# Output projection: its weight loads issued from ScalarE's queue

## Chip, cores and metric

One core of one Trainium2 chip runs the whole program. The metric is the device time of one execution in microseconds, the median of the runs shown.

## What is computed

One layer of a hybrid decoder for 2048 tokens of width 1024, in fp32. Cut to what matters here:

```python
hn = rms_norm(h, pre_mix_norm);  proj = hn @ w_in
o_a = gated_head_norm(gated_delta_rule_chunked(q, k, v, g, beta), gdn_norm, z)   # 4 heads of 128
o_b = gated_head_norm(hgrn2_chunked(q, k, i, log_f), hgrn_norm, g)               # 4 heads of 128
mix = concatenate([o_a, o_b])                       # (2048, 1024)
mix_out = mix @ w_out                               # the output projection
h = h + rms_norm(mix_out, post_mix_norm)
u = rms_norm(h, pre_mlp_norm) @ w_mlp_up            # MLP, 4096 wide
h = h + rms_norm(square(relu(u)) @ w_mlp_down, post_mlp_norm)
h = h + rms_norm(p @ w_ple_proj, ple_norm) * sigmoid(h @ w_ple_gate)
```

The change touches the loads of `w_out` alone.

## The kernel before

Everything is held transposed, channels on the 128 partitions and tokens along the free dimension, in four token quarters q of 512. Products are made to about fp32 precision with three matmuls per 128-channel block: each operand x is split into a high part (rounded to fp32r, ScalarE, `split` line 164) and the rest (VectorE, line 165), and high*high, high*low and low*high are summed in PSUM.

The order of TensorE's instructions is written out by hand for the whole program (`manual_schedule`). For the other engines a scheduler orders the instructions of the first part of the program, the output projection included, from its own estimate of when each is ready; SyncE's order is by hand in the mixing loop and again from the MLP on (line 1406), and left to the scheduler in between. Each engine, and each engine's DMA queue, takes its instructions in order: one that waits holds up those behind it. SyncE issues nearly all DMAs and computes nothing. GpSimd issues 16 accumulating ones.

The stages around the change:

- The end of the mixing: the last heads' recurrences (small matmuls with copies by ScalarE and VectorE between them), interleaved with the embedding projections (`mme`, copy `e` at line 307, store `ed` at line 309).
- The output projection, L1354 on: 32 tiles `(q, d)`, 8 columns d of 128 for each of 4 quarters q, 24 matmuls each (`mmo`, line 1143, the first two tiles at line 1100). Its moving operand `mixT` is loaded from DRAM (line 327) and split in place (lines 217 and 218). Each result is copied out by ScalarE (`yo`, L1392) and squared (`sq_o`, L233) for the norm that follows.
- Its weights: for q = 0 to 2 (`RAW = 3`) `stage_out(j)` loads a 128x1024 block of 512 KB into a `raw` buffer (two of them, line 338), and `ready_out(j)` splits it into a `whl` buffer (three of them). For q = 0 it also stores the split block to a DRAM cache (`keep`, line 180). For q = 3 `ready_out` reloads the split block, 1 MB, from the cache (`reload`, line 185), with no engine's work. In the loop over tiles, `ready_out(j + 2)` and `stage_out(j + 3)` come ahead of tile j's matmuls.
- The norms after each quarter: `hl` split, two `nrm` matmuls (lines 1174 and 1175), Ln and Exp on ScalarE with a table load before each (lines 1179, 1180), VectorE steps, then for q = 0 and 1 the residual: GpSimd's accumulating DMA adds x to `yo` (L1229), ScalarE squares the sum (`sq_h`, L233; `acc_h`, L226) and SyncE stores it (`h1d`, L1232). For q = 2 and 3 `yo` is stored (`yod`, L1396).
- The first operands of the MLP (`be`, `b`, `t`) are prepared while the last tiles run.

`reload` also serves the input projection, where its calls are unchanged.

Of the kernel before, what the change touches and what calls it, by code (L numbers as in the profile page):

```python
# [10 lines left out]
F32 = mybir.dt.float32  # L11
# [77 lines left out]
def trunk(ctx, tc, x, xT, pT, vecs, w_in, w_ab, gdn_a_log, gdn_dt_bias, w_out, w_up, w_down,  # L89
          w_ple, w_gate, consts, out):  # L90
    nc = tc.nc
    V, S, G, PE = nc.vector, nc.scalar, nc.gpsimd, nc.tensor
# [69 lines left out]
    def split(t, eng, raw):  # L162

        S.activation(t[:, 0], raw, AF.Copy)  # L164
        eng.tensor_tensor(t[:, 1], raw, t[:, 0], ALU.subtract)  # L165
# [9 lines left out]
    cached, sumd = {}, {}  # L175

    def keep(key, w):

        c = dr.tile([P, 2 * KD * P], F32, name=f"cache_{key}")
        nc.sync.dma_start(c, w.bitcast(F32).rearrange("p h k n -> p (h k n)"))  # L180
        cached[key] = c

    def reload(key, name):
        w = wp.tile([P, 2, KD, P], F32R, tag="whl", name=f"w_{name}")
        nc.sync.dma_start(w.bitcast(F32).rearrange("p h k n -> p (h k n)"), cached[key])
        return w

    def gemm(ps, terms):
# [143 lines left out]
    order = [(q, d) for q in range(NQ) for d in range(KD)]  # L332
    staged_out, ready, RAW = {}, {}, 3

    def stage_out(j):
        if j < len(order) and order[j][0] < RAW:
            raw = wp.tile([P, KD, P], F32, tag="raw", name=f"raw_out{j}", bufs=2)
            nc.sync.dma_start(raw, w_out[order[j][1]])
            staged_out[j] = raw

    def ready_out(j):
        if j >= len(order):
            return
        if j not in staged_out:
            ready[j] = reload(f"out{order[j][1]}", f"out{j}")
            return
        ready[j] = wp.tile([P, 2, KD, P], F32R, tag="whl", name=f"w_out{j}")
        split(ready[j], V, staged_out.pop(j))
        if order[j][0] == 0:
            keep(f"out{order[j][1]}", ready[j])  # L350
# [84 lines left out]
    with mixers as mctx:  # L435
# [538 lines left out]
        def split_work(j):  # L974

            if j < len(works):
                split_w[j] = staged.pop(j)() if j in staged else reload(works[j][1], works[j][0])
# [74 lines left out]
        with tc.manual_schedule(engines={mybir.EngineType.SP}):  # L1052
# [5 lines left out]
            for j, (name, key, src, q, h, then, g, b) in enumerate(works):  # L1058
# [4 lines left out]
                w, xt = split_w.pop(j), xts[q]  # L1063
# [20 lines left out]
            accs, store = {q: None for q in qs}, None  # L1084
            at(clock[0], mix_operands(0), (1, 2, 3, 4, 6, 7, 9, 11))
            call(clock[0] + 2, partial(stage_out, 0))
            call(clock[0] + 5, partial(ready_out, 0))
            call(clock[0] + 6, partial(stage_out, 1))
            call(clock[0] + 13, partial(ready_out, 1))
            call(clock[0] + 14, partial(stage_out, 2))  # L1090
            held = {}

# [261 lines left out]
    for j, (q, d) in enumerate(order):  # L1354
        if d == 0:
# [3 lines left out]
            if q == 1:  # L1359
                later(mix_operands(3), range(17, 25))  # L1360
        ready_out(j + 2)
        stage_out(j + 3)
        if j == len(order) - 5:
# [391 lines left out]
    for half in range(2):  # L1755
# [4 lines left out]
        for d in range(KD):  # L1760
            w = gated.pop((half, d))
# [70 lines left out]
```

## Time and profile before

| | us |
|---|---|
| median of 3 runs | 2715.93 |
| lowest and highest | 2712.65, 2716.56 |
| the profiled execution, first to last instruction (span) | 2719.9 |

The profiled execution's time is its span; nothing more than the span is given for it, and it lies 4.0 us above the median. Times in the prediction's rows count from the start of that span. The output projection runs from about 1113 to 1314 us. Rows of a timeline give start, duration, engine, line, operation, destination and source, and in brackets how long the engine stood idle before and what released it. `SPq` is SyncE's DMA queue; a row of it is the issue of a DMA, not its transfer. `xN` counts instructions that are merged in a row.

### The profile page before, as it was taken

To read this page: it belongs to the slowest core of one execution; us is meant where nothing else is said; L and a number is where in the kernel's file an instruction comes from. 1 tells how busy PE (TensorE), PEld (TensorE's weight loads), DVE (VectorE), ACT (ScalarE), POOL (GpSimd) and SP (SyncE) were. 2 spreads that over 40 slices of the span, in tenths; PEclk is the share of its full clock that TensorE was granted. 3 is DMA by queue.
4 is the path that set the end of the run, shared out by engine and by line. 5 is a ranking of instruction groups with operands and counts; after the bars stand their busy time and mean duration, and the time that the engine had idled before them with its cause. 6 is when DMAs were issued, how large, how long until landed. Compare 5 with 4: busy or idle time off the path is not lost.

```text
span 2719.9 us, 38475 instructions
## 1 busy us (share of the span) xinstructions
PE 2660.8 (98%) x12745; PEld 2215.1 (81%) x12745; DVE 2040.8 (75%) x4219; ACT 1464.0 (54%) x2940; POOL 118.5 (4%) x133
## 2 busy tenths in 40 slices
PE   8999999999999999998999999999999999999999
PEld 6788888888888887876788888888888888888887
DVE  7778878787777777576989867768787765567776
ACT  7665555465445455575655646555555545465432
POOL 0000000000000000011000000001000000001000
PEclk9999999999999999998999999999999999999999
DMA  8777777667666665887566457667454346577663
GB/s 282 273 237 255 236 263 242 216 214 241 213 201 221 223 213 164 271 281 231 177 232 228 175 178 240 216 202 244 164 196 163 139 172 207 193 256 247 216 212 131
DMA packets 268742, 589.24 MB, mean 217 GB/s; under 512 B 55658, under 2 KB 60232, under 8 KB 249344
## 3 DMA queue, kind: packets, MB, share of 16 engines
q1 hardware_dynamic: 266240, 582.59, 63.9%
q0 software_dynamic: 2304, 4.20, 0.9%
q8 instruction: 101, 1.65, 0.3%
q14 instruction: 97, 0.79, 0.1%
HBM read 419.75 MB, written 166.92 MB: 216 GB/s over the span
## 4 chain that ended last, share of the span: by engine, by line
PE 51%; DMA 3%; DVE 3%; issue 3%; ACT 1%; POOL 1%; SPq 0%; POOLq 0%; DVEq 0%; ACTq 0%
PE d L1143 22%; PE u L1143 22%; PE mmg L1143 6%; PE mmo L1143 1%; DMA raw_out<-in_w_out_dram 1%; DMA yo<-in_xT_dram 0%; PE mme L191 0%; POOL acc_y L234 0%; DMA b<-h1d 0%; DMA w_out<-cache_out 0%; DMA db<-hid 0%; DVE t L165 0%; DMA h1d<-yo 0%; POOL yo L1229 0%; DVE pr_g L698 0%
## 5 line engine op out<-in xcount | busy, mean ns | idle before, releaser
L1072 PE MATMUL mm<-xt,w 128*128 128x512 f32 x3072 | 784.1, 400 | 1.4 <-ACT zt_zg L577 1.1
L1072 PEld LDWEIGHTS mm<-xt,w 128*128 128x128 f32 x3072 | 553.3, 189 | 102.3 <-ACT zt_zg L577 1.5
L1143 PE MATMUL d<-db,da 128*128 128x512 f32 x2688 | 611.0, 389 | 0.5 <-ACT db L217 0.2
L1143 PE MATMUL u<-t,wu 128*128 128x512 f32 x2604 | 591.1, 389 | 0.0
L1143 PEld LDWEIGHTS d<-db,da 128*128 128x128 f32 x2688 | 504.3, 188 | 106.4 <-DVE db L218 1.0
L1143 PEld LDWEIGHTS u<-t,wu 128*128 128x128 f32 x2604 | 488.7, 188 | 101.5
L218 DVE TENSOR_TENSOR db<-db 128x512 fp32r<-128x512 f32 x224 | 159.9, 714 | 72.4 <-ACT db L217 71.7
L1495 DVE TENSOR_TENSOR u<-u,u 128x512 f32<-128x512 f32 x224 | 150.2, 681 | 58.1 <-PE u L1143 56.6
L1143 PE MATMUL mmo<-mixT,w_out 128*128 128x512 f32 x720 | 173.4, 402 | 11.8 <-DMA w_out<-cache_out 5.5
L217 ACT ACTIVATE db<-db 128x512 fp32r<-128x512 f32 x224 | 140.9, 629 | 78.2 <-DMA db<-hid 71.9
L1143 PEld LDWEIGHTS mmo<-mixT,w_out 128*128 128x128 f32 x720 | 139.5, 195 | 44.6 <-DMA w_out<-cache_out 5.9
L1143 PE MATMUL mmg<-h2T,wg 128*128 128x512 f32 (+1 forms) x792 | 174.8, 383 | 0.0
L1538 ACT ACTIVATE u<-u 128x512 f32<-128x512 f32 x128 | 80.8, 631 | 166.3 <-DVE u L1495 166.0
L1143 PEld LDWEIGHTS mmg<-h2T,wg 128*128 128x128 f32 x792 | 145.5, 188 | 29.1
L165 DVE TENSOR_TENSOR da<-da 128x512 fp32r<-128x512 f32 x128 | 93.7, 732 | 77.7 <-ACT da L164 77.1
L164 ACT ACTIVATE da<-da 128x512 fp32r<-128x512 f32 x128 | 80.5, 629 | 124.8 <-DMA da<-sumd 91.6
L164 ACT ACTIVATE wu<-a 128x512 fp32r<-128x512 f32 x124 | 75.0, 623 | 44.3 <-DMA a<-in_w_up_dram 43.0
L698 DVE TENSOR_TENSOR pr_g<-xs_g,sys_g 128x16 f32<-128x16 f32 (+14 forms) x240 | 94.4, 393 | 5.6
L165 DVE TENSOR_TENSOR wu<-a,wu 128x512 fp32r<-128x512 f32 x124 | 85.6, 693 | 10.8 <-ACT wu L164 10.5
L234 POOL TENSOR_TENSOR acc_y<-acc_y,sq_y 128x512 f32<-128x512 f32 x28 | 38.5, 1374 | 1261.6 <-ACT sq_y L233 1260.8
L1539 ACT ACTIVATE u<-u 128x512 f32<-128x512 f32 x128 | 80.5, 629 | 3.1
L165 DVE TENSOR_TENSOR da<-dr,da 128x512 fp32r<-128x512 f32 x96 | 66.3, 691 | 19.0 <-ACT da L164 16.5
(385 smaller groups left out, 3792.6 us busy)
## 6 DMA issues: line engine op xcount, KB each, us to landing
w<-cache_in SPq DMA_DIRECT2D x96, 1024.0 KB
db<-hid SPq DMA_DIRECT2D x224, 256.0 KB
cache_in<-w SPq DMA_DIRECT2D x32, 1024.0 KB
hid<-u SPq DMA_DIRECT2D x128, 256.0 KB
da<-sumd SPq DMA_DIRECT2D x128, 256.0 KB
a<-in_w_up_dram SPq DMA_DIRECT2D x124, 256.0 KB
hid<-ht SPq DMA_DIRECT2D x96, 256.0 KB
dr<-in_w_down_dram SPq DMA_DIRECT2D x96, 256.0 KB
```

The source lines that it names most:

```text
L164: S.activation(t[:, 0], raw, AF.Copy)
L165: eng.tensor_tensor(t[:, 1], raw, t[:, 0], ALU.subtract)
L217: S.activation(t[:, 0], plain(t), AF.Copy)
L218: V.tensor_tensor(t[:, 1], plain(t), t[:, 0], ALU.subtract)
L234: eng.tensor_tensor(acc, acc, sq, ALU.add)
L698: V.tensor_tensor(pr[:, :, :, 0:i], xs[:, None, :, 0:i].broadcast_to([P, 2, GC, i]), sys[:, 0:i, i : i + 2].rearrange("p j two -> p two j" ...
L1072: PE.matmul(ps, *terms[i], start=i == 0, stop=i == nt - 1)
L1143: PE.matmul(ps, a, b, start=start, stop=stop)
L1495: V.tensor_tensor(c[new], c[old], ps, ALU.add)
L1538: S.activation(c[k], c[k], AF.Relu)
L1539: S.activation(c[k], c[k], AF.Square)
```

## The change

All loads of the output projection's weights are issued by ScalarE: the 24 whole blocks in `stage_out` (512 KB each) and the 8 reloads of cached split ones in `ready_out` (1 MB each). `S` is `nc.scalar`. Addresses, sizes, buffers and splits stay.

```diff
-    def reload(key, name):
+    def reload(key, name, queue=None):
         w = wp.tile([P, 2, KD, P], F32R, tag="whl", name=f"w_{name}")
-        nc.sync.dma_start(w.bitcast(F32).rearrange("p h k n -> p (h k n)"), cached[key])
+        (queue or nc.sync).dma_start(w.bitcast(F32).rearrange("p h k n -> p (h k n)"), cached[key])
         return w
...
     def stage_out(j):
         if j < len(order) and order[j][0] < RAW:
             raw = wp.tile([P, KD, P], F32, tag="raw", name=f"raw_out{j}", bufs=2)
-            nc.sync.dma_start(raw, w_out[order[j][1]])
+            S.dma_start(raw, w_out[order[j][1]])
             staged_out[j] = raw
...
         if j not in staged_out:
-            ready[j] = reload(f"out{order[j][1]}", f"out{j}")
+            ready[j] = reload(f"out{order[j][1]}", f"out{j}", S)
             return
```

TensorE's and GpSimd's orders come out the same as before. ScalarE's has 32 rows more, SyncE's 32 less and some of its other DMAs, the `mixT` loads above all, stand earlier; on ScalarE and VectorE some instructions around the loads change places.

## The prediction

> **What bounds the kernel now.** I read the page first, then the time by windows around the output projection, then who waited for whom on TensorE, then the timelines of SyncE, ScalarE, VectorE and TensorE side by side. Tiles of the output projection are counted j = 8q + d, 0 to 31; j = 0 to 23 are loaded whole and split, j = 24 to 31 come back split from the cache.
>
> ```profile
> span 2719.9 us, 38475 instructions
> PE 2660.8 (98%) x12745; PEld 2215.1 (81%) x12745; DVE 2040.8 (75%) x4219; ACT 1464.0 (54%) x2940; POOL 118.5 (4%) x133
> 1060.00:1080.00 20.00, 16.66 (x85) 13.75 (x84) 15.98 (x40) 9.51 (x20) 0.00 (x0) 0.94 0.25 64
> 1140.00:1160.00 20.00, 20.00 (x90) 16.47 (x88) 8.73 (x12) 8.03 (x14) 1.01 (x1) 1.00 0.93 334
> 1160.00:1180.00 20.00, 17.63 (x71) 13.96 (x70) 11.77 (x16) 16.83 (x25) 0.00 (x0) 0.91 0.85 299
> 1240.00:1260.00 20.00, 16.67 (x61) 12.91 (x60) 15.12 (x23) 11.40 (x20) 4.52 (x6) 0.83 1.03 274
> 1260.00:1280.00 20.00, 14.53 (x53) 11.49 (x52) 5.10 (x9) 8.54 (x13) 0.00 (x0) 0.83 0.82 301
> PE mmo L1143 <- DMA w_out<-cache_out: 5.5, 1, 5.5
> PE mmo L1143 <- DVE w_out L165: 3.3, 3, 2.2
> PE mmo L1143 <- ACT w_out L164: 2.9, 2, 1.8
> SPq L338 <- DVE w_out L165: 19.2, 9, 3.6
> ```
>
> The window rows give length, then busy time and count of PE, PEld, DVE, ACT and POOL, the granted clock, the DMA share and GB/s. TensorE is busy 98% of the span, so only its gaps can be won or made. The undisturbed stretch 1140 to 1160 holds 90 matmuls, 0.222 us each and 5.33 us for a tile's 24. The three disturbed stretches hold 71, 61 and 53, so they lose 19, 29 and 37 matmuls: 4.2, 6.4 and 8.2 us, 18.8 us in all. That is more than the waits (11.7 us) because the granted clock falls to 0.91 and 0.83 beside them. 18.8 us is 0.7% of the span, the most that this stage can give. All three waits are for the weights whose loads are moved. The last row shows how they come late: SyncE's queue stood 19.2 us at the loads (L338), for VectorE to free the buffer.
>
> **The change part by part.** The compared orders show TensorE and GpSimd unchanged. 32 issues leave SyncE, 24 of 512 KB and 8 of 1 MB, and stand in ScalarE's order; the scheduler also moves the mixT loads ahead on SyncE and reorders some splits on ScalarE and VectorE.
>
> *The issues themselves.* No trace row shows an issue from ScalarE; the nearest are the same ones from SyncE.
>
> ```profile
> L338 SPq DMA_DIRECT2D raw_out<-in_w_out_dram x24: 332/414/1615, 1076.6 to 1239.6; - x24
> L185 SPq DMA_DIRECT2D w_out<-cache_out x8: 319/399/1712, 1258.2 to 1298.5; - x8
> ```
>
> At the medians 24 x 0.414 + 8 x 0.399 = 13.1 us of ScalarE over some 220 us; at the longest 1.6 and 1.7 us, 52 us. It is 54% busy, and the windows above leave it idle 3 to 12 us in 20, so I put the issues themselves at nothing; the waits and places below carry the price. Every whole load waits for VectorE's subtraction of the tile two earlier. On ScalarE that wait now holds the copies (yo), squares and splits queued behind it, for about one subtraction (1.2 us), less where mixT splits stand between.
>
> *Tile 8, the first gap.*
>
> ```profile
> 1147.40 1.23 DVE L165 TENSOR_TENSOR w_out<-raw_out,w_out 128x1024 fp32r<-128x1024 f32 x1 [1.59 <-ACT w_out L164]
> 1153.43 1.61 SPq L338 DMA_DIRECT2D raw_out<-in_w_out_dram  x1
> 1161.02 1.06 ACT L164 ACTIVATE w_out<-raw_out 128x1024 fp32r<-128x1024 f32 x1
> 1162.13 0.73 PE L1143 MATMUL mmo<-mixT,w_out 128*128 128x512 f32 x2 [1.85 <-ACT w_out L164]
> 1163.39 10.35 PE L1143 MATMUL mmo<-mixT,w_out 128*128 128x512 f32 x38 [0.53 <-DVE w_out L165]
> ```
>
> The buffer for tile 8 was free at 1147.40 + 1.23 = 1148.6, but SyncE, in order, came to the load at 1153.4. In the new order the load stands right behind ScalarE's copy of tile 6 and waits for this subtraction alone. The loads before it also go out sooner (tile 2's sits in ScalarE's order before the third embedding copy, near 1071). Walking the rows, tile 8 goes out near 1147 instead of 1153.4. A load then took 7.6 us to its copy, so the copy can begin near 1155, and with 2.3 us for copy and subtraction the weights are ready at 1157, before TensorE ends tile 7 at 1160.3. The gap closes: -4.2 us. Bounds: 0 (the load lands 4 us later) and -4.2 us.
>
> *Tile 23, the second gap.* Its cause is not the issue:
>
> ```profile
> 1247.54 0.63 ACT L233 ACTIVATE sq_h<-yo 128x512 f32<-128x512 f32 x1 [4.73 <-DMA yo<-in_xT_dram]
> 1249.03 1.06 ACT L164 ACTIVATE w_out<-raw_out 128x1024 fp32r<-128x1024 f32 x1
> 1253.12 7.86 PE L1143 MATMUL mmo<-mixT,w_out 128*128 128x512 f32 x22 [2.25 <-DVE w_out L165]
> ```
>
> The copy of tile 23 stands on ScalarE behind a square that waits for GpSimd's accumulating DMA, and the new order keeps it there. I put this at nothing, with -6.4 us (the gap goes) and +1.5 us (that DMA shares the engines with one queue more) as ends, the latter about the third of the 4.73 us that one competitor more of three would take.
>
> *Tiles 24 to 31, the third gap.*
>
> ```profile
> 1252.40 0.58 ACT L1392 ACTIVATE yo<-mmo 128x512 f32<-128x512 f32 x1
> 1258.18 0.42 SPq L185 DMA_DIRECT2D w_out<-cache_out  x1
> 1266.44 6.65 PE L1143 MATMUL mmo<-mixT,w_out 128*128 128x512 f32 x16 [5.47 <-DMA w_out<-cache_out]
> 1273.58 0.63 ACT L164 ACTIVATE hl_o<-acc_o 128x512 fp32r<-128x512 f32 x1 [5.38 <-PE nrm_h L1175]
> 1279.01 0.59 ACT L226 ACTIVATE acc_o<-mmo 128x512 f32<-128x512 f32 x1
> 1283.10 0.63 ACT L1179 ACTIVATE r_o<-acc_o 128x512 f32<-128x512 f32 x1 [2.21 <-DVE acc_o L1178]
> 1287.71 0.62 ACT L164 ACTIVATE t<-b 128x512 fp32r<-128x512 f32 x1
> ```
>
> TensorE ends tile 23 at 1253.12 + 7.86 = 1260.98. The reload of tile 24 went out at 1258.18 and let it go on at 1266.44, L = 8.26 us. Now it stands behind the copy and square of tile 21: about 1253.9. Idle before tile 24 is then L - 7.1. The later reloads are worse placed than on SyncE. Tile 27's stands behind the norm's Ln and Exp: from hl_o to the end of acc_o is 6.0 us, and hl_o waits for the norm's matmuls, 16 matmuls into tile 24 (1265.0), so it issues at 1271.0 where tile 27 is due at 1277.9: idle L - 6.9. Tile 28's stands behind the second Ln and Exp, from 1279.60 to 1287.71, 8.1 us and one issue later: 1279.5, with tile 28 due at 1283.2: idle L - 3.7, less what tile 27 has idled. Tiles 25, 26 and 29 to 31 have two tiles' time, 10.7 us, less some 2 us of ScalarE, which covers L up to about 8.5 us.
>
> L is the unknown. From below it is the fastest 512 KB load, plus its second half at the 301 GB/s of the row above (1.7 us); from above the slowest 512 KB load:
>
> ```profile
> 1163.36 0.33 SPq L338 DMA_DIRECT2D raw_out<-in_w_out_dram  x1
> 1166.85 1.06 ACT L164 ACTIVATE w_out<-raw_out 128x1024 fp32r<-128x1024 f32 x1 [0.60 <-DMA raw_out<-in_w_out_dram]
> 1194.45 0.67 SPq L338 DMA_DIRECT2D raw_out<-in_w_out_dram  x1
> 1204.74 1.06 ACT L164 ACTIVATE w_out<-raw_out 128x1024 fp32r<-128x1024 f32 x1 [1.53 <-DMA raw_out<-in_w_out_dram]
> ```
>
> That is 3.5 + 1.7 = 5.2 us and 10.3 us. I take the middle of 5.2 and 8.26, 6.7 us, since the reload no longer stands behind SyncE's stores. Idle is then 3.0 us, all before tile 28. The old gap lost 8.2 us for 5.47 idle, 1.5 for 1, so 3.0 costs 4.5: -3.7 us. At L = 5.2 it is -6.0, at 8.26 +0.5 (idle 5.8), at 10.3 +6.5 us (idle 9.8).
>
> The Trainium skill, page "DMA: Bandwidth & Descriptors", section "Issuing engines are not separate DMA queues", holds that DMAs from several engines share the same 16 DMA engines and that issuing from more of them only saves sequencer time. By it L would stay at the old value and the third gap would not shrink. No run so far tells the two apart: this trace has SyncE's queue and GpSimd's alone, and the 3.5 to 10.3 us are from one queue.
>
> *The end of the mixing.*
>
> ```profile
> 1067.45 0.43 ACT L826 ACTIVATE hb_h<-qk_h 128x256 f32<-128x256 f32 x1 [2.54 <-DVE qk_h L824]
> 1070.26 0.33 SPq L708 DMA_DIRECT2D xd_g<-xs_g  x1
> 1070.63 0.42 SPq L309 DMA_DIRECT2D ed<-e  x1
> 1074.83 0.60 ACT L307 ACTIVATE e<-mme 128x512 f32<-128x512 f32 x1 [4.32 <-DMA ed<-e]
> 1076.28 0.71 PE L853 MATMUL at_h<-qk_h,keys_h 128*128 128x128 f32 x4 [1.88 <-ACT keys_h L858]
> 1085.22 1.23 DVE L165 TENSOR_TENSOR w_out<-raw_out,w_out 128x1024 fp32r<-128x1024 f32 x1
> ```
>
> The loads of tiles 0 and 1 now go out near 1061. Tile 0's copy falls into ScalarE's idle 2.54 us before 1067.45 if the load lands in 3.5 us; if it takes 7.6, that cover is gone and the copies behind it slip by 1.6 us. Its subtraction (1.23 us) moves from 1085 into the solve that ends with the store xd_g, so xd_g, the store ed behind it on SyncE, the e copy and the keys behind that slip by about 0.9 us, and TensorE's 1.88 us wait grows by as much; at 1085 VectorE has 0.5 us less, since another split moves ahead there. Sum between -0.5 and +2.2, taken at +1.0 us.
>
> **Sum.** +1.0 - 4.2 + 0 - 3.7 = -6.9 us. The profiled span is 4.0 us above the median of the runs, 2715.93; the stage's difference is taken over to that median: 2709.0 us. About 0.2%, 5.4 us, is what a measurement of this kernel can tell from no change.
>
> **The rivals.** *Slower: the reloads wait behind ScalarE's own chain.* If reloads take as long as the slowest load, L = 10.3, tiles 24, 27 and 28 idle 3.2 + 3.4 + 3.2 us: +6.5; with the upper ends of mixing (+2.2) and tile 23 (+1.5) and tile 8's -4.2 it is +6.0, 2721.9 us. It decides from L = 8.2 up. For it: tile 28's issue 3.7 us before it is due. Against it: the DMA share of 0.82 and the clear queue.
>
> *No change: the DMA engines bound it.* The shares of 0.93, 0.85 and 1.03 speak for it; mixT loads move ahead into 1120 to 1160 and fill what was free. Tile 8's gap then stays, L = 8.26 (+0.5), mixing +1.0: +1.5, 2717.4 us. The rule of the Trainium skill above is this rival. Against it: tile 8 had its buffer 4.8 us before its load went out.
>
> *More: tile 23's gap goes too,* if the accumulating DMAs land earlier because SyncE's loads are out of the way: -6.9 - 6.4 = -13.3, 2702.6 us. Against it: the same bytes move in a window at 1.03.
>
> **How the numbers follow.** Forecast 0.45, slower 0.25, no change 0.17, more 0.13. The forecast's own range, -2 to -10 us, lies two thirds past -5.4: 0.31 faster, 0.14 same. "More" gives 0.13 faster; "no change" 0.02, 0.13, 0.02; "slower" 0.02 same, 0.23 slower. Together 0.46 faster, 0.29 same, 0.25 slower. Cases of both signs hold much, so the range goes past both outer ones by 3 us or so: 2699 to 2725; the likeliest alone 2706 to 2714.
>
> **What would show it.** Right: a second hardware queue of 20 MB, L338 and L185 on ScalarE's queue, 85 or more matmuls in the 20 us around tile 8, a wait of under 1 us before tile 24 and one of 2 to 4 us before tile 28. Wrong: the waits before tiles 24 to 28 sum over 6 us, a wait for w_out at tile 8, ScalarE standing for VectorE at L338 while TensorE waits for a free bank, or the end of the mixing losing over 3 us.

## Result and the profile after: slower by 0.29%

The changed kernel takes 2722.6 us, the median of 13 runs (2718.5 to 2728.2), the kernel before 2713.6 (2709.8 to 2720.0) beside it: ratio 1.0029 (the two medians alone give 1.0033), 95% interval 1.0021 to 1.0037, 5.7 to 10.0 us slower. 2709.0 and "faster" were forecast. The profiled execution of after took 2723.15 us, 1.85 more than its span. Medians of before differ by up to 10 us from one set of runs to the next, so below only ratios within a set are compared.

The page of after, and who waited for whom on TensorE and ScalarE between 1060 and 1340 us (total us, times, longest):

```profile
span 2721.3 us, 38491 instructions
q10 hardware_dynamic: 4608, 20.97, 2.4%
L338 ACTq DMA_DIRECT2D raw_out<-in_w_out_dram x24: 334/335/397, 1055.2 to 1242.9; - x24
PE mmo L1143 <- DVE w_out L165: 7.4, 3, 3.4
PE mmo L1143 <- DMA w_out<-cache_out: 5.4, 2, 5.0
PE psb_g L769 <- DVE r_g L766: 3.0, 1, 3.0
PE nrm_o L1174 <- ACT hl_o L164: 1.7, 3, 1.1
ACT yo L1392 <- DVE w_out L165: 5.9, 2, 5.0
ACT L1179 <- DVE w_out L165: 1.8, 1, 1.8
ACT hl_o L164 <- DVE w_out L165: 1.7, 1, 1.7
```

The change does what it says: a second hardware queue moves 21 MB, and an issue costs 0.335 us. New are a wait of the recurrence's `psb_g` for VectorE, and three kinds of waits of ScalarE for VectorE's weight splits, which are ScalarE standing at its own loads.

The spans differ by 1.4 us only, because after's execution came 4.8 us earlier to the first `mme` (1059.32 against 1064.12), in a part that the change leaves alone; over all the profiles below it comes between 1057.9 and 1067.4. So I count from there: the start of the first `mme`, then the start of the first matmul of tile n of the output projection (matmul 24n + 1 of `mmo`; all 768 are in every trace), then the last matmul of a norm in this stage (`nrm_o`, L1175; 1325.06 in before). The first line is in us from the first `mme`; the others are differences from it, so the change from one column to the next is what that stretch lost. Where TensorE waits for VectorE's half of a tile's weights, it does so ahead of that tile's third matmul, so such a wait counts in the next column. Single profiles of one order differ: e3 keeps before's order up to tile 23 and reads up to 2.2 us lower, e14 up to tile 9 and reads up to 1.0 us higher.

| kernel | tile 0 | 2 | 7 | 9 | 15 | 17 | 21 | 23 | 25 | norm |
|---|---|---|---|---|---|---|---|---|---|---|
| before | 49.1 | 63.3 | 90.6 | 105.8 | 138.9 | 150.3 | 173.5 | 186.0 | 211.1 | 260.9 |
| after | +3.0 | +4.0 | +4.0 | +3.3 | +5.3 | +5.7 | +8.9 | +7.7 | +5.2 | +6.4 |
| e1 | +2.3 | +3.3 | +3.3 | +1.5 | +4.8 | +8.0 | +8.1 | +6.8 | +7.7 | +7.6 |
| e2 | -0.8 | -0.8 | -0.8 | +0.7 | +1.2 | +1.2 | +1.7 | +0.1 | -5.2 | -3.9 |
| e3 | -1.9 | -1.9 | -1.9 | -1.9 | -1.9 | -1.9 | -1.0 | -2.2 | -0.8 | -0.2 |
| e4 | +3.7 | +3.2 | +3.9 | +1.9 | +7.5 | +8.7 | +9.8 | +9.1 | +1.7 | +11.4 |
| e5 | -0.4 | -0.6 | -0.6 | -2.3 | -2.3 | -2.3 | -1.4 | -2.4 | -1.2 | -0.4 |
| e6 | -0.7 | +0.3 | +0.3 | -3.8 | -0.9 | +1.4 | +5.6 | +4.0 | -0.2 | +0.1 |
| e7 | -0.9 | +2.0 | +3.1 | -1.3 | -1.3 | +1.0 | +3.6 | +1.9 | +0.3 | +0.5 |
| e8 | +6.4 | +6.0 | +7.1 | +4.8 | +9.6 | +10.0 | +12.6 | +10.9 | +11.5 | +13.3 |
| e9 | +1.9 | +3.4 | +3.4 | +0.1 | +2.5 | +3.3 | +6.6 | +4.9 | +3.4 | +4.1 |
| e10 | -1.0 | +0.2 | +0.2 | +1.7 | +5.1 | +5.8 | +9.1 | +7.4 | +6.1 | +6.8 |
| e11 | +1.2 | +1.6 | +4.2 | +7.9 | +7.9 | +7.9 | +7.7 | +6.5 | +7.2 | +6.9 |
| e12 | -0.1 | +0.3 | +2.8 | +6.7 | +6.7 | +6.7 | +6.8 | +5.1 | +0.3 | +0.9 |
| e13 | -0.5 | +1.8 | +1.8 | -2.5 | -0.6 | +2.6 | +2.4 | +1.5 | +0.1 | +0.5 |
| e14 | +0.8 | +0.8 | +1.0 | +1.0 | +1.0 | +1.0 | +4.5 | +2.9 | +1.6 | +2.2 |
| e15 | -0.8 | +0.7 | +0.7 | -3.7 | -0.8 | +2.4 | +5.0 | +3.5 | -0.3 | -0.5 |

After loses 3.0 us by tile 0 and 1.0 behind it; it wins 0.7 from tile 7 to 9, loses 2.0 on the way to 15, 0.4 to 17 and 3.2 from 17 to 21; it wins 3.7 from 21 to 25 and loses 1.2 to the end: 6.4 us, beside 7.9 measured.

### The profile page after: what moved, and what is told of

It reads as the page before. It is cut to its first block, busy times and chain, and to the rows that moved or that the text cites. A ratio compares the mean times of both kernels' runs of the same rounds, so it can differ in the third digit from the quotient of the medians.

```text
span 2721.3 us, 38491 instructions
## 1 busy us (share of the span) xinstructions
PE 2657.6 (98%) x12745; PEld 2212.0 (81%) x12745; DVE 2040.5 (75%) x4219; ACT 1463.6 (54%) x2940; POOL 119.3 (4%) x133
## 4 chain that ended last, share of the span: by engine, by line
PE 56%; DVE 5%; DMA 4%; issue 4%; ACT 1%; POOL 1%; SPq 0%; POOLq 0%; DVEq 0%; ACTq 0%
PE u L1143 22%; PE d L1143 21%; PE mmg L1143 6%; PE mm L1072 4%; PE mmo L1143 1%; DVE pr_g L698 1%; POOL acc_y L234 0%; DMA rsb_g<-rd_g 0%; DMA mixT<-mixd 0%; DVE t L165 0%; PE mme L191 0%; DMA sys_g<-ud_g 0%; DVE xs_g L701 0%; DMA yo<-in_xT_dram 0%; DMA ud_g<-u_g 0%
```

## The experiments

### Which loads: e1 to e4

The `raw` load is issued from ScalarE where the condition holds, else from SyncE (e1 `j < KD`, e2 `j >= KD`); `reload` stays on SyncE in both. e3 is the reverse. e4 takes GpSimd for all.

```diff
-            S.dma_start(raw, w_out[order[j][1]])
+            (S if j < KD else nc.sync).dma_start(raw, w_out[order[j][1]])     # e1
+            (nc.sync if j < KD else S).dma_start(raw, w_out[order[j][1]])     # e2
+            nc.sync.dma_start(raw, w_out[order[j][1]])                        # e3, reload on S
+            G.dma_start(raw, w_out[order[j][1]])                              # e4, reload on G
```

> Only the eight whole weights of the first block of 512 tokens are loaded from ScalarE's queue; the other sixteen and the cached ones stay on SyncE's. Theory A (order): the two first loads, free of SyncE's order, land some 20 us earlier, the scheduler then puts their splits ahead of the operands of the mixing's end, and SyncE's freed places go to later transfers ahead of the last heads' norms; most of the loss sits here, from the trace of after 3.0 us at the end of the mixing, 1.0 at a low clock behind it and little at the tiles 7 and 8: slower by 3 to 6 us, about 2718. Theory B (ScalarE stands at each load until VectorE has freed the buffer): a third of the loads, a third of the loss, some 2 to 3 us. Theory C (a second hardware queue slows the small transfers of SyncE's): about 2 us, where both queues are busy at the end of the mixing.

Measured: 1.0036 (1.0023 to 1.0048). The first eight alone lose as much as the whole change, more than the 3 to 6 us expected, but in part elsewhere: 3.3 us by tile 2, and 6.5 us from tile 9 to 17, where after loses 2.4.

> Only the sixteen whole weights of the second and third block are loaded from ScalarE's queue; the first eight and the cached ones stay on SyncE's. Theory A: no order of the mixing's end is touched, so the 4 us there are not lost, and what is left is ScalarE held ahead of the rows of the norms and of tile 20, 1 to 3 us slower in the trace of after, less up to 3 us if the gap before tile 23 closes: within 2 us of before. Theory B: two thirds of the loads, so about 5 us slower. Theory C: about 4 us slower.

Measured: 0.9992 (0.9983 to 1.0001). The later sixteen lose nothing, against B and C.

> Only the eight cached split weights are loaded from ScalarE's queue; all whole ones stay on SyncE's. Theory A: the order changes only from tile 23 on; in the trace of after tile 24 still waited 5.0 us, and the stretch from tile 23 to tile 32 was 3.1 us shorter than before: 0 to 3 us faster, about 2712. Theory B: the first load stands behind a copy that waits for its buffer's store, nothing gained, 0 to 1 us slower. Theory C: 1 to 2 us slower, all three waits of tiles 24, 27 and 28 longer by the second queue's landings.

Measured: 1.0008 (0.9999 to 1.0017). No gain; the reload still came late (below).

> All 32 loads are issued from GpSimd's queue, which does little else here; ScalarE issues none. SyncE is freed of them just as in after, so the order of SyncE and most of that of VectorE is new in the same way. Theory A: the loss stays for the most part, slower than before by 3 to 8 us, unless the first splits come where they were. Theory B: ScalarE no longer stands at a load, so the loss goes: within 2 us of before or faster by up to 7. Theory C: the loads still run on a queue of their own, slower by 4 to 8 us.

Measured: 1.0067 (1.0053 to 1.0081), the worst of all. With nothing issued by ScalarE the loss is larger, and 3.7 us of it are lost by tile 0 with a wait of 1.5 us for `r_g`, so ScalarE's standing is not the whole of it. GpSimd stands in its turn: 87.8 us in 18 waits at the loads, for VectorE's subtractions. Its own instructions are not held up by that: every power step of the norms (`m_h`, `m_e`, `m_g`) in this stage begins within 0.3 us of the end of VectorE's step before it. The profile shows 11.4 of the 18 us measured in this stage, 9.7 of them behind tile 25, where TensorE waits 5.9 us for the split of a weight of the MLP (`w_u`); why that comes late was not taken apart.

### Why the first loads cost: e5 to e8

At the end of the mixing the two kernels agree until the last 2 us: `mme` 15 of 16 (groups of six matmuls) begins 0.2 us earlier in after than in before, counted from the first. Then VectorE of after, and of before:

```profile
1104.77 0.16 DVE L280 TENSOR_SCALAR m_e<-m_e 128x4 f32<-128x4 f32 x1
1108.36 0.75 DVE L593 SCALAR_TENSOR_TENSOR og_g<-og_g,cols,rsb_g 128x512 f32<-128x512 f32 x1 [3.43 <-DMA rsb_g<-rd_g]
1110.23 0.34 DVE L766 SCALAR_TENSOR_TENSOR r_g<-vt_g,inv_g,psa_g 128x128 f32<-128x128 f32 x1
1110.63 0.49 PE L769 MATMUL psb_g<-r_g,xt_full 128*128 128x128 f32 x2 [3.01 <-DVE r_g L766]
```

```profile
1111.33 0.35 DVE L766 SCALAR_TENSOR_TENSOR r_g<-vt_g,inv_g,psa_g 128x128 f32<-128x128 f32 x1
1112.64 0.75 DVE L593 SCALAR_TENSOR_TENSOR og_g<-og_g,cols,rsb_g 128x512 f32<-128x512 f32 x1 [0.96 <-DMA rsb_g<-rd_g]
```

In before the recurrence's `r_g` comes first and the norm's product `og_g`, which waits for the landing of `rsb_g`, after it. In after they have changed places, and TensorE stands 3.01 us. Nothing in the diff names either. Counted from the first `mme`, the loads of the first two weights go out 16.6 and 28.8 us sooner and the first weight's subtraction comes 16.2 us sooner, and the scheduler places the rest anew by its estimates; e5 shows that the early loads alone are enough to turn the pair.

```diff
# e5, from before                            # e8, from after, in ready_out
-  call(clock[0] + 2, partial(stage_out, 0))  +  if j == 0:
+  stage_out(0)                               +      V.tensor_copy(ready[0][:, 0, 0, :1],
-  call(clock[0] + 6, partial(stage_out, 1))  +                    xin[0][1][:, 0, :1])
+  stage_out(1)                                  split(ready[j], V, staged_out.pop(j))
# e6, from after; e7 has the reloads on SyncE besides
+  (nc.sync if j < 3 else S).dma_start(raw, w_out[order[j][1]])
```

> The kernel before, all loads on SyncE's queue, with its first two whole weights issued at the start of the mixing's end instead of 2 and 6 steps later. No second queue and no load on ScalarE. VectorE's order then has the norm's product og_g, which waits for rsb_g, ahead of the recurrence's r_g, as in after; in the kernel before r_g comes first. Theory A (order): the stretch from the first mme to tile 0, 49.1 us before, 48.2 and 47.2 in the two runs that kept its order, 51.4 to 52.8 where the first eight loads moved, takes 50 to 52 us, with a wait of 1.5 to 3 us for r_g at its end; the kernel is slower by 1 to 5 us, about 2717. Theory B (ScalarE stands at the loads) and theory C (a second hardware queue): none of it, 47 to 49 us, within 1.5 us of before.

Measured: 0.9999 (0.9990 to 1.0007), 48.7 us to tile 0. A miss for theory A in size: `og_g` stands ahead of `r_g` here too, but its row had nearly landed.

```profile
1114.16 0.75 DVE L593 SCALAR_TENSOR_TENSOR og_g<-og_g,cols,rsb_g 128x512 f32<-128x512 f32 x1 [1.23 <-DMA rsb_g<-rd_g]
1114.83 0.34 DVE L766 SCALAR_TENSOR_TENSOR r_g<-vt_g,inv_g,psa_g 128x128 f32<-128x128 f32 x1
1115.23 0.49 PE L769 MATMUL psb_g<-r_g,xt_full 128*128 128x128 f32 x2 [0.91 <-DVE r_g L766]
```

So the bad order is not enough; the price is how late the landing is behind it, 0.9 us here and 3.0 in after. From `rsb_g`'s issue to its use took 4.7 us here, 4.6 in before, 5.6 in after and 4.9 to 5.2 in e1, e4, e6 and e7, of which e6 and e7 had no load on a second queue yet: for this row a longer landing beside a second queue (C) is at most 1 us and not shown.

> As after, but the first three whole weights are loaded from SyncE's queue as before; the other 21 and the cached ones stay on ScalarE's. Theory A: the order at the end of the mixing is that of before, so 47 to 49 us to tile 0 and no wait for r_g; the later stretch as in after, which lost 2.4 us from tile 2 on, so 0 to 3 us slower than before, about 2716. Theory B: 21 of 24 loads still stand on ScalarE, so six or seven of the eight us stay, 2721. Theory C: likewise 5 to 8 us.

Measured: 1.0007 (0.9998 to 1.0016), 48.4 us to tile 0 and no wait for `r_g`. With the first three loads back on SyncE, some 6 of the 7.9 us are gone (1.0029 to 1.0007): 3.7 us by tile 0 and 3.4 from tile 7 to 9 in the table.

> As the one from tile 3 on, with the cached weights back on SyncE's queue. Theory A: the gap before tile 24 shrinks as in the run of the later sixteen alone (1.6 us against 5.5), worth 4 to 6 us, and tiles 7 and 8 may lose or win 2: 1 to 5 us faster than before, about 2712. Theory B: 5 to 7 us slower. Theory C: 3 to 6 us slower.

Measured: 0.9993 (0.9984 to 1.0002). By the two ratios the cached loads cost some 4 us on ScalarE's queue, but the intervals overlap and the two profiles end within 0.4 us of each other: not shown.

> After, with one more instruction: the first weight's split is held until the second mixing operand is split, by a copy of one column (128x1) into the weight's place. All loads stay on ScalarE's queue and as early as in after, but VectorE's order has r_g ahead of og_g again. Theory A: the wait of 3.0 us for r_g at the end of the mixing goes and the stretch from the first mme to tile 0 takes 48 to 50.5 us instead of 52.1; the kernel is 2 to 4 us faster than after, still 3 to 6 slower than before. Theories B and C: both causes stay, 51 to 53 us and no faster than after.

Measured: 1.0035 (1.0023 to 1.0047), 55.5 us to tile 0 (+6.4). The wait for `r_g` went as expected, the time did not: another waiting row of the same kind took its place.

```profile
1115.39 0.17 DVE L280 TENSOR_SCALAR m_e<-m_e 128x4 f32<-128x4 f32 x1 [3.59 <-DMA m_e<-sd_e]
1116.07 0.34 DVE L778 SCALAR_TENSOR_TENSOR S_g<-S_g,cd_g,psc_g 128x128 f32<-128x128 f32 x1
1116.47 0.49 PE L766 MATMUL psa_g<-S_g,y_kg 128*128 128x128 f32 x2 [1.77 <-DVE S_g L778]
```

VectorE waits for `m_e` ahead of `S_g`; 16 us earlier it waited 2.57 us for `rsb_h` in the same way. TensorE's wait of 1.77 us is only part of the 6.4; the rest was not taken apart. Since every edit gives the scheduler's order a new form, the theory is tested better by taking the waiting instruction off VectorE.

### Taking the waiting instruction away: e9 to e12

```diff
-            V.scalar_tensor_tensor(og, og, col(...), rsb, ALU.mult, ALU.mult)
+            if n in ("g3_2",):            # e9; e10 to e12: ("g3_2", "h3_3", "g3_3")
+                G.tensor_tensor(og, og, rsb, ALU.mult)
+                G.tensor_scalar(og, og, col(...), None, ALU.mult)
+            else: ...
```

e9 and e10 start from after, e11 from before, e12 from e2.

> After, with one product moved: og_g of head 2 in the last block, the instruction that waits for rsb_g ahead of r_g in VectorE's order, is done on GpSimd as two instructions (128x512 by the row, then by the column of gains). All 32 loads stay on ScalarE's queue. Theory A2 (the loss at the end of the mixing is VectorE standing in order at an instruction that waits for a landing, ahead of the recurrence): the 3.0 us wait for r_g goes, 48 to 50.5 us from the first mme to tile 0 where after had 52.1, and the kernel is 2 to 5 us faster than after, 1.001 to 1.002 of before. Theory B (ScalarE standing at its loads) and theory C (small transfers land later beside a second queue, 5.6 us from issue to use for rsb_g against 4.6 before): the wait turns up elsewhere, 51 to 53 us, and the ratio stays 1.003.

Measured: 1.0012 (1.0001 to 1.0022), 4.6 us less than after by the two ratios. To tile 0 it took 51.0 us, half a microsecond over what was expected, but the wait is gone:

```profile
1113.86 0.35 DVE L770 SCALAR_TENSOR_TENSOR r_g<-vt_g,inv_g,psa_g 128x128 f32<-128x128 f32 x1 [1.35 <-PE psa_g L768]
1115.04 0.39 PE L773 MATMUL psb_g<-r_g,xt_full 128*128 128x128 f32 x2
1116.31 1.29 POOL L594 TENSOR_TENSOR og_g<-og_g,rsb_g 128x512 f32<-128x512 f32 x1 [2.66 <-DMA rsb_g<-rd_g]
1116.43 2.26 DVE L165 TENSOR_TENSOR w_out<-raw_out,w_out 128x1024 fp32r<-128x1024 f32 x1 [0.26 <-ACT w_out L164]
```

VectorE has `r_g` done 2.1 us before GpSimd has its row and begins the product, and TensorE doesn't wait. From the start of the last group of six `mme` to tile 0 the kernel after loses 3.2 us against before, e9 0.1 and e10 0.1: so much is the product's. The 1.9 us that e9 still loses by tile 0 come from the solve ahead of it, a slip that after had and made up. By the table only 1.1 us of e9's gain on after stand at tile 0 and 0.6 at tile 2; most of it, 2.6 us, comes from tile 7 to 9, where the last head's row took 4.0 us from issue to use (6.8 in after), an instruction that e9 leaves where it was. So the 4.6 us are not the price of this one product alone.

> After, with the three last such products of the last block (heads g 2, h 3 and g 3) on GpSimd. Theory A2: besides the wait for r_g, the gap at tile 7 (3.4 us for VectorE's subtraction, which stood behind og_g waiting 4.3 us) falls under 1.5 us; together 4 to 7 us faster than after, 1.000 to 1.002 of before. Theory B: the copies and rows held by ScalarE remain, no more than 2 us gained on after. Theory C: the landings stay late, so the second operands are late too; no more than 2 us gained.

Measured: 1.0039 (1.0025 to 1.0052). At the end of the mixing the whole loss is gone (48.1 us to tile 0, -1.0), as A2 says, and the wait at tile 7 is 0.49 us instead of 3.39; then TensorE waits 4.96 us before tile 9, and by tile 15 5.1 us are lost. SyncE, which stands at the store of GpSimd's product with the `mixT` loads behind it, holds ScalarE for 10 us, and tile 9's split stands behind that:

```profile
1163.44 0.32 SPq L599 DMA_DIRECT2D mixd<-og_g  x1
1170.30 1.31 ACT L217 ACTIVATE mixT<-mixT 128x512 fp32r<-128x512 f32 x2 [10.01 <-DMA mixT<-mixd]
1173.58 6.64 PE L1147 MATMUL mmo<-mixT,w_out 128*128 128x512 f32 x14 [4.96 <-ACT w_out L164]
```

> The kernel before, all loads on SyncE's queue, with the same three products on GpSimd. Every other order stays as before but for one neighbouring pair on VectorE. Theory A2: the wait of 5.3 us for rsb_h and of 1.5 for rsb_g leave VectorE's order, so the splits of tiles 3 to 8 come earlier and the gap at tile 8 (1.9 and 0.5 us, with a low clock behind it) goes at least in part: 1 to 4 us faster than before. Theories B and C say nothing of VectorE's order here: the load on SyncE and its landing set tile 8, within 1 us of before.

Measured: 1.0030 (1.0017 to 1.0042): a miss, for the same reason. GpSimd and SyncE of e11:

```profile
1160.72 1.30 POOL L594 TENSOR_TENSOR og_g<-og_g,rsb_g 128x512 f32<-128x512 f32 x1 [7.97 <-DMA rsb_g<-rd_g]
1162.12 2.94 POOL L595 TENSOR_SCALAR og_g<-og_g,cols 128x512 f32<-128x512 f32 x1
1156.95 0.32 SPq L180 DMA_DIRECT2D cache_out<-w_out  x1
1165.09 0.32 SPq L599 DMA_DIRECT2D mixd<-og_g  x1
1173.76 6.56 PE L1147 MATMUL mmo<-mixT,w_out 128*128 128x512 f32 x20 [5.32 <-ACT w_out L164]
```

GpSimd ends the product at 1165.06, where VectorE takes 0.75 us for it. SyncE stands from 1157 to 1165 at its store, with loads of weights and operands behind it, and TensorE waits 5.3 us for `w_out` at tile 8. The wait was not removed but moved from VectorE's order to SyncE's.

> The later sixteen whole loads on ScalarE's queue, the first eight and the cached ones on SyncE's, and the three products on GpSimd. If the gains add up: the later sixteen alone measured 0.9992 of before, with tile 24's wait 1.6 us instead of 5.5, and the products 1 to 4 us more: 3 to 7 us faster than before, 0.9975 to 0.999. If GpSimd's products delay the stores of the mixed rows so that the last block's operands are late, or tile 23's wait of 3.5 us takes up the gain: within 2 us of before.

Measured: 1.0011 (0.9998 to 1.0023). No sum of gains; TensorE waits 5.0 us in the middle of tile 8, for a split of `mixT`.

### Tiles 7 to 21: e13 to e15

The conditions for ScalarE are `3 <= j < 8`, `16 <= j`, and both, with the reloads on SyncE.

> Only the whole weights of tiles 3 to 7 are loaded from ScalarE's queue, all others from SyncE's. Theory D (ScalarE standing at a load until VectorE has freed its buffer costs where a norm's row or a split is queued behind it): tiles 8 to 23 are not on ScalarE, so the 2.5 us that the runs from tile 3 on lost between tiles 15 and 21 are gone (under 1 us), while the gap at tile 8 closes (3 us won between tiles 7 and 9): 1 to 4 us faster than before. Theory E (the scheduler's new order of the residual's squares and stores is what costs there): the 2.5 us stay or turn up elsewhere, within 1.5 us of before.

Measured: 1.0009 (1.0001 to 1.0018). 1 to 4 us faster was expected. From 17 to 21 nothing is lost (-0.2), against 3.2 in after and 2.6 to 4.2 in e6, e7 and e15. The gap at tile 8 closes (-4.3 from 7 to 9). But 3.2 us go from 15 to 17, where tile 16's weights come late; e1, e6, e7 and e15 lose 2.3 to 3.2 us there too, after 0.4. That loss was not taken apart.

> Only the whole weights of tiles 16 to 23 are loaded from ScalarE's queue. Theory D: the norm of the second quarter falls between these loads, so 1 to 2 us are lost between tiles 16 and 21; freed of them, SyncE comes to the reload of tile 24 earlier and the gap before it shrinks by 2 to 5 us: within 3 us of before, rather faster. Theory E: no loss between tiles 16 and 21, 2 to 5 us faster.

Measured: 0.9997 (0.9988 to 1.0006); 3.5 us lost from 17 to 21. This is theory D, with ScalarE of e14 showing it:

```profile
1221.72 0.33 ACTq L338 DMA_DIRECT2D raw_out<-in_w_out_dram  x1
1222.11 0.63 ACT L164 ACTIVATE hl_o<-acc_o 128x512 fp32r<-128x512 f32 x1 [1.67 <-DVE w_out L165]
1222.79 0.50 PE L1174 MATMUL nrm_o<-hl_o,ones 128*128 128x512 f32 x1 [1.52 <-ACT hl_o L164]
```

The load waits for VectorE to free its buffer; the norm's split `hl_o`, right behind it, goes out 0.4 us after it, and TensorE waits 1.52 us for that. After's rows at 1219 are the same (1.67 us, and 1.14 at TensorE). But the loads alone don't make the loss. e2 has tiles 16 to 23 on ScalarE too and loses 0.5 us from 17 to 21; in its order the norm's split stands behind no load that waits:

```profile
1214.71 0.62 ACT L164 ACTIVATE hl_o<-acc_o 128x512 fp32r<-128x512 f32 x1
1217.40 0.50 PE L1175 MATMUL nrm_o<-hl_o,ones 128*128 128x512 f32 x1 [0.17 <-DVE hl_o L165]
```

> The whole weights of tiles 3 to 7 and 16 to 23 are loaded from ScalarE's queue. If the parts add up: 3 us at tile 8, 2 to 5 us at tile 24, less 1 to 2 us between tiles 16 and 21: 3 to 6 us faster than before, 0.998 to 0.999. If not, within 2 us of before as the run of tiles 3 to 23 was (0.9993).

Measured: 1.0006 (0.9997 to 1.0015). The parts come out in the stage, -4.4 from 7 to 9 and -5.3 from 21 to 25, but +6.1 from 9 to 17 and +2.6 from 17 to 21 take the gain up. No version beat the kernel before by more than its interval; e2 and e7, 0.9992 and 0.9993, came nearest.

## Why the prediction was wrong, step by step

The prediction summed to -6.9 us, the profile of after shows +6.4: 13.3 us apart. In the table 3.0 of them lie at the end of the mixing, up to tile 2 (+4.0 for +1.0), 3.5 at tile 8 (-0.7 for -4.2), 5.6 from tile 9 to 21 (+5.6 for 0) and 1.2 from there to the end (-2.5 for -3.7). So three steps failed.

**The end of the mixing (+1.0, at most +2.2) failed in its path.** It lost 3.0 us, and 1.0 more behind it, while the first eight matmuls of tile 0 took 3.24 us at a granted clock of 0.56 where the same eight take 1.98 us at tile 1 at 1.00:

```profile
1111.42 3.24 PE L1100 MATMUL mmo<-mixT,w_out 128*128 128x512 f32 x8
1120.11 1.98 PE L1100 MATMUL mmo<-mixT,w_out 128*128 128x512 f32 x8
```

The prediction followed the early split into the solve, and that slip did happen (+2.2 us at the seventh group of `mme`) and was made up again. What it did not follow is the order that the scheduler gave to `og_g` and `r_g` behind it, which stood in the compared orders all along. e9 and e10 show it: with the one product off VectorE the 3.2 us between the last `mme` and tile 0 are gone.

**Tile 8 (-4.2, bound 0): the mechanism holds, the forecast doesn't.** Where the first three loads stay on SyncE and those of tiles 3 to 7 move, the gap closes, -4.1 to -4.4 us from tile 7 to 9 in e6, e7, e13 and e15. In after only 0.7 us is won, because the wait is at tile 7 instead (the last row is before's, for the same product):

```profile
1155.35 0.75 DVE L593 SCALAR_TENSOR_TENSOR og_g<-og_g,cols,rsb_g 128x512 f32<-128x512 f32 x1 [4.27 <-DMA rsb_g<-rd_g]
1156.62 1.22 DVE L165 TENSOR_TENSOR w_out<-raw_out,w_out 128x1024 fp32r<-128x1024 f32 x1
1157.87 0.35 ACTq L338 DMA_DIRECT2D raw_out<-in_w_out_dram  x1
1158.27 0.60 ACT L1392 ACTIVATE yo<-mmo 128x512 f32<-128x512 f32 x1 [4.96 <-DVE w_out L165]
1157.89 14.59 PE L1143 MATMUL mmo<-mixT,w_out 128*128 128x512 f32 x62 [3.39 <-DVE w_out L165]
1151.15 0.75 DVE L593 SCALAR_TENSOR_TENSOR og_g<-og_g,cols,rsb_g 128x512 f32<-128x512 f32 x1 [1.49 <-DMA rsb_g<-rd_g]
```

ScalarE had copied tile 7's weights at 1151.2. VectorE's half stood behind `og_g`, waiting 4.27 us for the last head's row. SyncE issued that row's load at 1148.54, 89.2 us from the first `mme` where before has 82.4, and it took 6.8 us from issue to use, 4.6 in before. It is the mechanism of the mixing's end once more, and ScalarE stands with it, 4.96 us at its load. e10 takes this wait away (0.49 us). Why the row lands later is open: 6.3 to 9.1 us in after, e6, e7, e8, e13 and e15, which load tiles 3 to 7 from ScalarE, and 3.7 to 5.0 in before, e2, e3, e5 and e14, which load them from SyncE, speak for theory C here; 4.7 in e1 and 4.0 in e9, with the same loads on ScalarE, speak against it.

**The loads' waits on ScalarE (nothing) cost about 3 us.** An issue is 0.335 us and hidden, as said. The wait at L338 was foreseen too ("about one subtraction": 1.67 to 1.77 us in the norms' rows), but it was put at nothing, though the norm's split lies on the path to TensorE. e13 and e14 price it: 3.5 us lost from tile 17 to 21 with the loads of 16 to 23 on ScalarE, 0.2 won without, and 3.2 lost in after. e2 limits this: with another order the same loads cost 0.5 us. Of the 2.0 us that after lost from tile 9 to 15, 1.2 are two waits of the first quarter's norm for its split `hl_o` (0.36 and 0.84 us, none in before); what held that split was not taken apart.

**Tiles 23 and 24 (0 and -3.7) came out by luck.** After won 3.7 us from tile 21 to 25, the number forecast, but hardly by shorter waits: ahead of tiles 23 and 24 TensorE waited 8.3 us in all in after and 8.8 in before. The rest is TensorE's rate: the last 22 matmuls of tile 23 took 7.86 us at a granted clock of 0.65 in before (first row) and 5.28 at 1.00 in after.

```profile
1253.12:1260.98 7.86, 7.85 (x22) 5.95 (x22) 6.26 (x10) 3.90 (x7) 0.00 (x0) 0.65 1.00 334
1257.00:1262.28 5.28, 5.28 (x22) 4.05 (x22) 3.83 (x7) 2.41 (x5) 0.00 (x0) 1.00 0.97 317
```

L was right: 6.7 us from the reload of tile 24, 6.4 from that of tile 28. But the wait is before tile 24 (4.96 us, forecast under 1) and not before tile 28 (0.45, forecast 3.0):

```profile
1258.79 0.60 ACT L1392 ACTIVATE yo<-mmo 128x512 f32<-128x512 f32 x1 [3.79 <-DMA yod<-yo]
1260.54 0.37 ACTq L185 DMA_DIRECT2D w_out<-cache_out  x1
1267.24 6.25 PE L1143 MATMUL mmo<-mixT,w_out 128*128 128x512 f32 x16 [4.96 <-DMA w_out<-cache_out]
1292.99 22.04 PE L1143 MATMUL mmo<-mixT,w_out 128*128 128x512 f32 x96 [0.45 <-DMA w_out<-cache_out]
```

The reload was to go out behind the copy `yo` of tile 21, 7.1 us before TensorE ended tile 23. That copy waited 3.8 us for an earlier store of its buffer (`yod`), which SyncE issues, and the reload went out 1.7 us before. In e3 the reload itself stood on ScalarE, 4.6 us for the landing of a load of SyncE's; in the trace both of these transfers count on one completion counter, and the reload waits for it:

```profile
1253.58 0.35 ACTq L185 DMA_DIRECT2D w_out<-cache_out  x1
1253.98 0.63 ACT L164 ACTIVATE t<-be 128x512 fp32r<-128x512 f32 x1 [4.60 <-DMA u_raw<-in_w_up_dram]
```

What helped was SyncE freed of the whole loads: in e2, with the reloads on SyncE, the wait is 1.6 us and the stretch from tile 21 to 25 6.9 us shorter. How sure a single profile is here: in e5 and e11, whose order at this place is before's, the wait is 9.9 and 9.8 us against before's 5.5. Nor does the wait give the loss, as the forecast's 1.5 us lost for 1 us idle supposed: e5 waited some 3.5 us more than before at tiles 23 and 24 and took only 0.2 us longer from 21 to 25, with its 22 matmuls in 5.28 us like after.

**The rivals.** The forecast's slower rival gave 2721.9, near what came, for another reason: L was 6.7, not 10.3. The second queue gave reloads no clearly shorter time: from the issue of tile 24's to its first matmul 6.7 to 8.2 us on ScalarE's queue (after, e3, e6, e8 to e10), 6.9 to 8.9 on SyncE's (before, e1, e2, e5, e7, e11 to e15). That agrees with the rule of the Trainium skill that the prediction weighed (page "DMA: Bandwidth & Descriptors", section "Issuing engines are not separate DMA queues"), that another issuing engine saves sequencer time only; but it is not what decided here. The rival of no change, which rests on that rule, was priced at +1.5 us.

## What to carry to other kernels

Moving a DMA to another queue moves its waits, too: whatever is queued behind it on the new engine waits for its buffer and for its completion counter. Where a scheduler orders the rest, read the new order of every engine for instructions that wait for a landing and now stand ahead of a chain that the busiest engine needs; here that list, more than the diff, carried the price. When such a wait is taken off one engine, ask whose order it joins next.

## What was not expected of the hardware

While GpSimd did the product of e9 (1.29 and 2.42 us), VectorE's 128x1024 subtraction took 2.26 us instead of 1.23, and in e11 1.95; beside the product by a column alone one took 1.21 (e10). The Trainium skill, page "GPSIMD Engine Reference", section "8. Key points", names it: GpSimd shares its SBUF interfaces with VectorE and contends with instructions of two SBUF inputs. GpSimd took 1.3 us for a 128x512 product by a row, but 1.6 to 2.9 us for one by a column, which has fewer inputs; VectorE does both at once in 0.75. The same issue cost 0.335 us from ScalarE, 0.414 from SyncE and 0.542 from GpSimd (medians of 24).
